# Two-head attention on one core: loads in halves, casts shared out and transposes moved in the first pair of heads

## The chip, the cores and the metric

The kernel runs on one core of a Trainium2 chip. The metric is the time of one execution in microseconds (us) of device time; lower is better. Three runs of the kernel before gave a median of 118.17 us (118.06 to 118.36). A separate execution was profiled: it took 117.7 us, of which the profile covers a span of 115.9 us; all times "at 5.19" in this document count from the start of that span.

## The reference

Softmax attention over 8 x 8 = 64 heads, 512 positions and 64 columns each, all in float32:

```python
def reference(q, k, v):                      # each (8, 8, 512, 64) float32
    scale = 1.0 / np.sqrt(q.shape[-1])
    scores = np.einsum('bhqd,bhkd->bhqk', q, k) * scale
    scores = scores - scores.max(axis=-1, keepdims=True)
    attn = np.exp(scores)
    attn = attn / attn.sum(axis=-1, keepdims=True)
    return np.einsum('bhqk,bhkd->bhqd', attn, v).astype(np.float32)
```

The inputs are drawn from a normal distribution with a fixed seed. The kernel leaves the subtraction of the maximum out, which changes nothing in exact arithmetic; it gets the row sums from a column of ones beside v.

## The kernel before, in words

Heads are worked on in 32 pairs (g = 0 to 31). For each pair one DMA each brings q, k and v (256 KB each, 128 partitions; a partition holds four neighbouring rows of each head, that is 1,024 contiguous bytes a head). Casts to float16 follow, mostly on POOL (GpSimd); PE (TensorE) transposes 128x128 blocks of q and k into PSUM, DVE (VectorE) copies these to SBUF, and PE multiplies them into scores. A *group* m is two score blocks of 128 keys by 512 queries, which share one of three PSUM buffers (st0, st1, st2). ACT (ScalarE) takes the exponential of a whole group in one instruction (128x1024, L594) and writes it to SBUF as float16. For 12 of the groups, from m = 11 on, DVE computes the exponential itself with a polynomial (L612, L634) so that ACT does not have to. PE then multiplies the exponentials with v (L683, "values"), and DVE normalises by the row sums (L655, L663) before the result is stored.

A class `Plan` simulates the engines once, with fixed costs and due times, when the program is built; the order of all steps after the start is its list. Each engine runs its own instructions strictly in the order of the program text, with semaphores between engines. The list that `Plan` makes is the same before and after the change.

The first pair (g = 0) is written by hand, in `first_loads` and `first_pair`. Its parts, which the prediction refers to:

- *Loads.* ACT's queue issues two loads of k (head 0, head 1; L727), SP's queue two loads of q (L728), each 128 KB. SP then goes on with the loads of the pairs 1 to 6 and part of 7 (L498), one after the other.
- *Casts.* q is cast into `q16` with every row written twice, side by side (`twice`), so that its transpose holds q in partitions 0 to 63 and again in 64 to 127. Head 0: q rows 0 and 1 on DVE (L746), k rows 0 and 1 on DVE (L747), q rows 2 and 3 on ACT (L748), k rows 2 and 3 on POOL (L749). Head 1: k on ACT (L750), q on POOL (L751). ACT loads its table of functions (L748, ACT_TABLE_LOAD) after it has issued its loads.
- *Fillers.* `busy` (L732) multiplies a constant, into a buffer that is overwritten later; it only keeps PE active. Six of 512 columns and two of 128 stand in front of the transposes, three of 128 in front of the first scores, and four of 128 in front of the scores of group 2.
- *Head 0.* Transposes of q blocks 0 and 1 into `tp_qa`, of k blocks 0 and 1 (L763; the first into `st_ka`, the second into buffer st1), of q blocks 2 and 3 into st1. Four DVE copies (L794 to L797) put them into `qt` and `kt`. Then the scores (L773): group 0 in two halves of 256 queries (`st_0a`, `st_0b`), each with an exponential of its own on ACT (L780), and group 1 (`st1`).
- *Head 1.* Four q transposes into `tp_qb`, two k transposes into `tp_kb`, the DVE copies L810 and L814, and the scores of group 2 (`st2`). The scores of group 3, the last of the pair, are the first step of `Plan`'s list (L589), followed by the transposes of pair 1 (L544, two times four), whose q half was cast in two parts on DVE (L512) and POOL (L513), the copies L551 and the scores of group 4, the first of pair 1.

Of the kernel before, what the change touches and what calls it, by code (L numbers as in the profile page):

```python
# [404 lines left out]
def kernel(  # L405
# [7 lines left out]
    nc = tc.nc  # L413
    B, H, S, D = q.shape
    P = 128
    NI = S // P
# [56 lines left out]
    def source(src, g):  # L473
        b, h = g // ppb, 2 * (g % ppb)
        return src[b, h : h + 2].rearrange("h (p i) d -> p h i d", i=NI)

    def load_tile(g, name):
        t = lpool.tile(
            [P, 2, NI, D],
            FP32,  # L480
            tag=f"{name}32",
            name=f"{name}32_{g}",
            bufs=7,
        )
        raw.setdefault(g, {})[name] = t
        return t
# [75 lines left out]
    def buffer(b, name):  # L562
        return ps_st.tile([P, 2, S], FP32, tag=f"st{b}", name=name)

    def scores(m, on_dve, b):
        grp = groups[m]
        half = m - len(groups) + 2
        cols = slice(256 * half, 256 * half + 256) if half >= 0 else slice(0, S)
        st = buffer(b, f"st_{m}")
        if on_dve:  # L570
            bits = dpool.tile([P, 2, S], U32, tag="pd", name=f"pd_{m}")
            pt = bits.bitcast(FP16).rearrange("p x (s n) -> p x s n", n=2)[:, :, :, 0]
            for x, (_, _, h) in enumerate(grp):
                s = slice(64 * h, 64 * h + 64)
                nc.tensor.matmul(st[:, x, :], lift[s], ones[s, 0:S], start=True, stop=False)
        elif half == 1:
            pt = last["pt"]
        else:
            pt = last["pt"] = ppool.tile([P, 2, S], FP16, tag="pt", name=f"pt_{m}")
        for x, (g, c, h) in enumerate(grp):  # L580
            if g == 0:
                s = slice(64 * (c % 2), 64 * (c % 2) + 64)
                kc = first["kt"][s, h, c // 2, :]
                qc = first["qt"][s, h].rearrange("p i c -> p (i c)")
            else:
                s = slice(64 * h, 64 * h + 64)
                kc = tqk[g][s, 1, c * P : (c + 1) * P]
                qc = tqk[g][s, 0, :]
            nc.tensor.matmul(st[:, x, cols], kc, qc[:, cols], start=not on_dve, stop=True)  # L589
            blocks[(g, c, h)] = pt[:, x, :]  # L590
        if on_dve:
            raised[m] = {"st": st, "bits": bits}
            return
        nc.scalar.activation(  # L594
            out=pt[:, :, cols], in_=st[:, :, cols], func=EXP, scale=scale
        )
# [126 lines left out]
    def first_loads():  # L723
        tk = load_tile(0, "k")
        tq = load_tile(0, "q")
        for h in range(2):
            nc.scalar.dma_start(out=tk[:, h], in_=source(k, 0)[:, h])  # L727
            nc.sync.dma_start(out=tq[:, h], in_=source(q, 0)[:, h])  # L728

    def busy(dst, n):  # L730

        nc.tensor.matmul(dst[:, 0:n], ones[:, 0:P], ones[:, 0:n], start=True, stop=True)  # L732

    def first_pair():


        tk, tq = raw[0]["k"], raw[0]["q"]
        k16 = cpool.tile([P, 2, NI, D], FP16, name="k16_0")
        q16 = cpool.tile([P, 2, NI, 2, D], FP16, name="q16_0")
        kt = cpool.tile([P, 2, 2, P], FP16, name="kt_0")  # L740
        qt = cpool.tile([P, 2, NI, P], FP16, name="qt_0")

        def twice(h, i, n):
            return tq[:, h, i : i + n].rearrange("p i (x d) -> p i x d", x=1).broadcast_to([P, n, 2, D])

        nc.vector.tensor_copy(out=q16[:, 0, 0:2], in_=twice(0, 0, 2))  # L746
        nc.vector.tensor_copy(out=k16[:, 0, 0:2], in_=tk[:, 0, 0:2])  # L747
        nc.scalar.copy(q16[:, 0, 2:4], twice(0, 2, 2))  # L748
        nc.gpsimd.tensor_copy(out=k16[:, 0, 2:4], in_=tk[:, 0, 2:4])  # L749
        nc.scalar.copy(k16[:, 1], tk[:, 1])  # L750
        nc.gpsimd.tensor_copy(out=q16[:, 1], in_=twice(1, 0, NI))  # L751

        pka, st1, st0 = (buffer(b, f"st_{n}") for b, n in enumerate(("ka", "1", "0a")))
        pqa = ps_x.tile([P, 8, P], FP16, tag="x0", name="tp_qa")
        pqb = ps_x.tile([P, 8, P], FP16, tag="x1", name="tp_qb")

        pka, pkc, pqc = pka[:, 0, :], st1[:, 0, :], st1[:, 1, :]
        pka, pkc, pqc = (
            t.bitcast(FP16).rearrange("p (n c) -> p n c", c=P) for t in (pka, pkc, pqc)
        )  # L760

        def t_k(dst, h, j):
            nc.tensor.transpose(  # L763
                dst, k16[:, h, 2 * j : 2 * j + 2, :].rearrange("p i d -> p (i d)"), ident
            )

        def t_q(dst, h, i):
            nc.tensor.transpose(dst, q16[:, h, i].rearrange("p x d -> p (x d)"), ident)

        def first_scores(st, h, j, q0, q1, pt, s0, s1):  # L770
            for x in range(2):
                s = slice(64 * x, 64 * x + 64)
                nc.tensor.matmul(  # L773
                    st[:, x, s0:s1],
                    kt[s, h, j, :],
                    qt[s, h].rearrange("p i c -> p (i c)")[:, q0:q1],
                    start=True,
                    stop=True,
                )
            nc.scalar.activation(  # L780
                out=pt[:, :, q0:q1], in_=st[:, :, s0:s1], func=EXP, scale=scale
            )

        for n in range(6):
            busy(st0[:, 0], S)
        for n in range(2):
            busy(st0[:, 0], P)
        for i in range(2):
            t_q(pqa[:, i], 0, i)
        t_k(pka[:, 0], 0, 0)  # L790
        t_k(pkc[:, 0], 0, 1)
        for i in range(2):
            t_q(pqc[:, i], 0, 2 + i)
        nc.vector.tensor_copy(out=qt[:, 0, 0:2], in_=pqa[:, 0:2])  # L794
        nc.vector.tensor_copy(out=kt[:, 0, 0], in_=pka[:, 0])
        nc.vector.tensor_copy(out=qt[:, 0, 2:4], in_=pqc[:, 0:2])
        nc.vector.tensor_copy(out=kt[:, 0, 1], in_=pkc[:, 0])  # L797
        for n in range(3):
            busy(st0[:, 1], P)
        pts = [ppool.tile([P, 2, S], FP16, tag="pt", name=f"pt_{m}") for m in range(3)]  # L800
        for m in range(3):
            for x, b in enumerate(groups[m]):
                blocks[b] = pts[m][:, x, :]
        first_scores(st0, 0, 0, 0, 256, pts[0], 0, 256)
        st0b = buffer(0, "st_0b")
        first_scores(st0b, 0, 0, 256, 512, pts[0], 0, 256)
        first_scores(st1, 0, 1, 0, S, pts[1], 0, S)
        for i in range(NI):
            t_q(pqb[:, i], 1, i)
        nc.vector.tensor_copy(out=qt[:, 1], in_=pqb[:, 0:4])  # L810
        pkb = ps_x.tile([P, 8, P], FP16, tag="x0", name="tp_kb")
        for j in range(2):
            t_k(pkb[:, j], 1, j)
        nc.vector.tensor_copy(out=kt[:, 1], in_=pkb[:, 0:2])  # L814
        st2 = buffer(2, "st_2")
        for n in range(4):
            busy(st2[:, 0], P)
        first_scores(st2, 1, 0, 0, S, pts[2], 0, S)
        first.update(kt=kt, qt=qt)

    with tc.manual_schedule():
        plan = Plan(groups, NP, 3)
        steps = plan.run()
        first_loads()
        for g, name in plan.first_loads:
            load(g, name)
# [5 lines left out]
        for n in range(NV):  # L832
            nc.vector.memset(vps[n][:, :, :, D : D + 1], 1.0)
        first_pair()
        do = {
            "transposes": transposes,
            "scores": scores,
            "values": values,
            "load": load,
# [43 lines left out]
```

## Time and profile before

| | |
|---|---|
| median of three runs | 118.17 us (118.06 to 118.36) |
| profiled execution, own time | 117.7 us |
| its span | 115.9 us |
| busy in the span: ACT, PE, DVE, POOL | 94%, 91%, 88%, 68% |
| first exponential (L780) starts | 5.19 us |
| fourth exponential (group 2, L780) starts | 7.48 us |
| last exponential ends | 112.60 us |

The profile's "busy" leaves out waiting and DMA issue. On PE, consecutive matmuls overlap in the records: one record covers the whole passage through the array, so the distance from start to start tells how fast they follow. "PEld" is PE's loading of weights, which runs beside its matmuls. The same holds for exponentials on ACT: one of 128x1024 is recorded with some 1.02 us, and the next starts 0.904 us after it.

### The profile page before, as it was taken

The page shows a single profiled execution, that of the slowest core. Times are in us where ns is not written, and L with a number is a line of the kernel's source. Part 1 is how long each engine was busy: PE and PEld are TensorE (multiplying, and loading weights), DVE is VectorE, ACT ScalarE, POOL GpSimd, SP SyncE. Part 2 cuts the span into 40 slices and gives each one's busy share as a digit, 9 for nine tenths or more (in the row PEclk, how much of TensorE's full clock was granted, in tenths as well). Part 3 has the DMA queues.
Part 4 walks back from the last instruction along what each step waited for, and adds up shares of the span by engine and source line. Part 5 has one row for each costly group of instructions (what it writes and reads, how often), then busy time and mean ns, then how long its engine had stood idle before and what let it go on. Part 6 is the DMA issues. An engine that isn't in the chain of part 4 may idle for free.

```text
span 115.9 us, 4106 instructions
## 1 busy us (share of the span) xinstructions
PE 105.8 (91%) x1583; PEld 67.1 (58%) x1583; DVE 101.6 (88%) x180; ACT 109.1 (94%) x121; POOL 78.9 (68%) x122
## 2 busy tenths in 40 slices
PE   7979997999989998899979999999999999899980
PEld 2546563657557565476655565765666665567660
DVE  4463599999999999999999999999999999999381
ACT  4499999999999999999999999999999999999980
POOL 2579870895995799676946999679995598740000
PEclk9999999999999999999999999999999999999999
DMA  3999999999999999999996899999999972035354
GB/s 105 326 373 378 384 380 382 383 376 322 343 367 338 306 362 385 369 378 354 316 296 210 264 320 343 294 312 369 328 306 314 332 269 94 0 96 184 95 187 133
DMA packets 35604, 33.83 MB, mean 292 GB/s; under 512 B 2688, under 2 KB 35584, under 8 KB 35584
## 3 DMA queue, kind: packets, MB, share of 16 engines
q1 hardware_dynamic: 35152, 33.24, 86.5%
q10 hardware_dynamic: 432, 0.33, 0.9%
q8 instruction: 12, 0.20, 0.7%
q14 instruction: 8, 0.07, 0.1%
HBM read 25.17 MB, written 8.39 MB: 289 GB/s over the span
## 4 chain that ended last, share of the span: by engine, by line
ACT 28%; PE 20%; DVE 15%; POOL 12%; issue 12%; DMA 8%; SPq 3%; POOLq 0%; ACTq 0%
ACT pt L594 27%; PE o L683 7%; PE st L589 6%; DMA v<-in_v_dram 5%; POOL qkp L519 5%; DVE ring L663 4%; POOL vp L504 3%; PE st_0a L732 3%; DMA out_dram<-ring 3%; DVE tqk L557 2%; DVE y L634 2%; DVE z L612 2%; DVE pd L634 2%; POOL t L647 2%; POOL k L517 2%
## 5 line engine op out<-in xcount | busy, mean ns | idle before, releaser
L594 ACT ACTIVATE pt<-st 128x1024 f16<-128x1024 f32 (+1 forms) x114 | 104.1, 1075 | 0.1
L589 PE MATMUL st<-tqk 64*128 64x512 f16 (+1 forms) x250 | 46.1, 381 | 4.2 <-ACT pt L594 3.1
L683 PE MATMUL o<-vp,pt 128*128 128x65 f16 x912 | 43.1, 194 | 0.7 <-DVE ring L663 0.6
L683 PEld LDWEIGHTS <-pt 128*128 128x128 f16 x912 | 35.6, 98 | 13.0 <-issue 10.3
L504 POOL CAST vp<-v 128x512 f16<-128x512 f32 x32 | 19.2, 616 | 10.4 <-DVE pd L634 5.9
L519 POOL CAST qkp<-k 128x512 f16<-128x512 f32 x31 | 21.0, 678 | 4.7 <-PE o L683 2.5
L663 DVE TENSOR_TENSOR ring<-o,rc 128x448 f32<-128x448 f32 (+2 forms) x37 | 22.6, 611 | 1.1
L589 PEld LDWEIGHTS <-tqk 64*128 64x128 f16 x250 | 13.2, 93 | 17.4 <-issue 8.7
L557 DVE COPY tqk<-tp 128x1024 f16<-128x1024 f16 x30 | 20.3, 676 | 3.0 <-PE tp L544 3.0
L519 POOL CAST qkp<-q 128x512 f16<-128x512 f32 x30 | 19.4, 646 | 4.4 <-DVE pd L634 4.0
L544 PE MATMUL tp<-ident,qkp 128*128 128x128 f16 x248 | 19.6, 219 | 0.8 <-DVE ring L663 0.5
L544 PEld LDWEIGHTS <-qkp 128*128 128x128 f16 x248 | 14.2, 97 | 8.4 <-issue 3.6
L634 DVE SCALAR_TENSOR_TENSOR pd<-y,z 128x1024 uint32<-128x1024 f32 x12 | 14.9, 1246 | 0.0
L612 DVE TENSOR_SCALAR z<-st 128x1024 f32<-128x1024 f32 x12 | 14.6, 1218 | 0.2 <-PE st L589 0.2
L634 DVE SCALAR_TENSOR_TENSOR y<-st,z 128x1024 f32<-128x1024 uint16 x12 | 14.6, 1215 | 0.0
L683 PE MATMUL o<-vp,pd 128*128 128x65 f16 x96 | 14.5, 194 | 0.0
L683 PEld LDWEIGHTS <-pd 128*128 128x128 f16 x96 | 9.4, 98 | 1.4 <-issue 1.2
L655 DVE RECIPROCAL rc<-o 128x7 f32<-128x7 f32 (+2 forms) x37 | 7.3, 197 | 2.9 <-PE o L683 2.6
L650 POOL TENSOR_TENSOR y<-t,y 128x1024 f32<-128x1024 f32 x4 | 9.5, 2364 | 0.3
L517 POOL TENSOR_SCALAR k<-k 128x128 f32<-128x128 f32 x12 | 6.3, 528 | 1.8 <-DVE pd L634 1.2
L634 DVE SCALAR_TENSOR_TENSOR y<-z,y 128x1024 f32<-128x1024 uint16 x4 | 5.4, 1344 | 0.0
L634 DVE SCALAR_TENSOR_TENSOR y<-st,y 128x1024 f32<-128x1024 uint16 x4 | 4.9, 1216 | 0.0
(53 smaller groups left out, 37.8 us busy)
## 6 DMA issues: line engine op xcount, KB each, us to landing
out_dram<-ring SPq DMA_DIRECT2D x63, 128.0 KB, 3.8
k<-in_k_dram SPq DMA_DIRECT2D x31, 256.0 KB, 5.1
q<-in_q_dram SPq DMA_DIRECT2D x31, 256.0 KB, 5.1
v<-in_v_dram SPq DMA_DIRECT2D x27, 256.0 KB, 4.8
v<-in_v_dram SPq DMA_DIRECT2D x10, 128.0 KB, 3.6
k<-in_k_dram ACTq DMA_DIRECT2D x2, 128.0 KB, 2.9
q<-in_q_dram SPq DMA_DIRECT2D x2, 128.0 KB, 2.7
out_dram<-obl SPq DMA_DIRECT2D x1, 64.0 KB, 1.6
```

Source lines behind the costliest of these rows:

```text
L504: return nc.gpsimd.tensor_copy(out=vps[g % NV][:, :, :, 0:D], in_=raw[g]["v"][:, :, :, :])
L517: ins = nc.gpsimd.tensor_scalar(out=x, in0=x, scalar1=LOG2E, scalar2=None, op0=AluOp.mult)
L519: ins = nc.gpsimd.tensor_copy(out=dst, in_=src[:, :, :, :])
L544: nc.tensor.transpose(tps[g][:, n, i, :], qkp[g][:, n, i, :], ident)
L557: nc.vector.tensor_copy(out=tqk[g][:, :, :], in_=tps.pop(g).rearrange("p n i c -> p n (i c)"))
L589: nc.tensor.matmul(st[:, x, cols], kc, qc[:, cols], start=not on_dve, stop=True)
L594: nc.scalar.activation(out=pt[:, :, cols], in_=st[:, :, cols], func=EXP, scale=scale)
L612: nc.vector.tensor_scalar(out=r["z"][:, :, :], in0=r["st"][:, :, :], scalar1=128.0, scalar2=2.0**17, op0=AluOp.mult, op1=AluOp.max,)
L634: nc.vector.scalar_tensor_tensor(out=r["bits"][:, :, :] if last else y, in0=(low, one, y)[s], scalar=(QUARTIC if shared else CUBIC)[s], in ...
L650: nc.gpsimd.tensor_tensor(out=y[:, :, :], in0=t[:, :, :], in1=y[:, :, :], op=AluOp.mult)
L663: nc.vector.tensor_tensor(out=ring[:, u % NU : u % NU + n, :], in0=o[:, x : x + n, 0:D], in1=rc[:, 0:n].broadcast_to([P, n, D]), op=AluOp. ...
L683: nc.tensor.matmul(os[u // 7][:, u % 7, :], blocks[(g, c, h)][:, y * P : (y + 1) * P], vps[g % NV][:, h, c, :], start=(c == 0), stop=(c == ...
```

## The change

In the first pair only, except for the fillers of group 4:

- The loads of head 0's q and k are cut in halves: rows 0 and 1, then rows 2 and 3 of each partition's four (64 KB, 512 bytes a partition), so that each of the two queues issues three loads where it issued two.
- Head 1's q is cast in two halves, rows 0 and 1 on POOL and rows 2 and 3 on ACT, where POOL cast all of it. On ACT this half stands in front of the cast of head 1's k.
- Head 1's first q transpose stands in front of the scores of group 0; its other three, and the two of k, stand behind group 0's scores and in front of group 1's, where all six stood behind group 1's.
- Fillers: one of 128 columns fewer in front of head 0's transposes, one fewer in front of the first scores, two fewer in front of group 2's; six new ones of 128 columns in front of group 4's scores.

```diff
@@ scores(m, on_dve, b)
+        if m == 4:
+            for n in range(6):
+                busy(st[:, 0], P)
@@ first_loads()
-        for h in range(2):
-            nc.scalar.dma_start(out=tk[:, h], in_=source(k, 0)[:, h])
-            nc.sync.dma_start(out=tq[:, h], in_=source(q, 0)[:, h])
+        for h, i, n in ((0, 0, 2), (0, 2, 2), (1, 0, 4)):
+            nc.scalar.dma_start(out=tk[:, h, i : i + n], in_=source(k, 0)[:, h, i : i + n])
+            nc.sync.dma_start(out=tq[:, h, i : i + n], in_=source(q, 0)[:, h, i : i + n])
@@ first_pair()
         nc.gpsimd.tensor_copy(out=k16[:, 0, 2:4], in_=tk[:, 0, 2:4])
+        nc.gpsimd.tensor_copy(out=q16[:, 1, 0:2], in_=twice(1, 0, 2))
+        nc.scalar.copy(q16[:, 1, 2:4], twice(1, 2, 2))
         nc.scalar.copy(k16[:, 1], tk[:, 1])
-        nc.gpsimd.tensor_copy(out=q16[:, 1], in_=twice(1, 0, NI))
...
         for n in range(6):
             busy(st0[:, 0], S)
-        for n in range(2):
-            busy(st0[:, 0], P)
+        for n in (P,):
+            busy(st0[:, 0], n)
...
-        for n in range(3):
+        for n in range(2):
             busy(st0[:, 1], P)
+        for i in range(1):
+            t_q(pqb[:, i], 1, i)
...
         first_scores(st0b, 0, 0, 256, 512, pts[0], 0, 256)
-        first_scores(st1, 0, 1, 0, S, pts[1], 0, S)
-        for i in range(NI):
+        for i in range(1, NI):
             t_q(pqb[:, i], 1, i)
-        nc.vector.tensor_copy(out=qt[:, 1], in_=pqb[:, 0:4])
         pkb = ps_x.tile([P, 8, P], FP16, tag="x0", name="tp_kb")
         for j in range(2):
             t_k(pkb[:, j], 1, j)
+        first_scores(st1, 0, 1, 0, S, pts[1], 0, S)
+        nc.vector.tensor_copy(out=qt[:, 1], in_=pqb[:, 0:4])
         nc.vector.tensor_copy(out=kt[:, 1], in_=pkb[:, 0:2])
         st2 = buffer(2, "st_2")
-        for n in range(4):
+        for n in range(2):
             busy(st2[:, 0], P)
         first_scores(st2, 1, 0, 0, S, pts[2], 0, S)
```

The order of instructions on DVE, and all that follows `Plan`'s list, stays as it was; SP's list gains one load at its head.

## The prediction

> **What bounds the kernel now.** First the page's busy table and its groups, then the timeline of ACT after the start:
>
> ```profile
> PE 105.8 (91%) x1583; PEld 67.1 (58%) x1583; DVE 101.6 (88%) x180; ACT 109.1 (94%) x121; POOL 78.9 (68%) x122
> L594 ACT ACTIVATE pt<-st 128x1024 f16<-128x1024 f32 (+1 forms) x114 | 104.1, 1075 | 0.1
> 27.62 84.98 ACT L594 ACTIVATE pt<-st 128x1024 f16<-128x1024 f32 x93
> ```
>
> ACT is the busiest engine, and its 114 exponentials of L594 have 0.1 us of idle time between them, all told. The last row is one unbroken stretch from 27.62 to 112.60. So ACT runs without a gap from its first L594 on, and the kernel ends a fixed tail after it. A change of the first pair is worth what it moves the start of that stretch. The chain of waits passes DVE, POOL and DMA rows between 47 and 100, but ACT has no idle row there: those engines run beside it with buffers between.
>
> Next, the timeline from 3 to 10, ACT first, then the engines that feed it:
>
> ```profile
> 3.33 0.40 ACT L748 CAST q<-q 128x256 f16<-128x256 f32 x1 [0.42 <-DMA q<-in_q_dram]
> 4.21 0.41 ACT L750 CAST k<-k 128x256 f16<-128x256 f32 x1 [0.47 <-DMA k<-in_k_dram]
> 5.19 0.60 ACT L780 ACTIVATE pt<-st_0a 128x512 f16<-128x512 f32 x1 [0.58 <-PE st_0a L773]
> 6.17 1.03 ACT L780 ACTIVATE pt<-st 128x1024 f16<-128x1024 f32 x1
> 7.48 1.02 ACT L780 ACTIVATE pt<-st 128x1024 f16<-128x1024 f32 x1 [0.29 <-PE st L773]
> ...
> 3.53 0.38 POOL L749 CAST k<-k 128x128 f16<-128x128 f32 x1 [2.25 <-DMA k<-in_k_dram]
> 3.99 0.61 POOL L751 CAST q<-q 128x512 f16<-128x512 f32 x1
> 6.05 0.40 POOL L513 CAST qkp<-q 128x256 f16<-128x256 f32 x1 [0.21 <-DMA q<-in_q_dram]
> ...
> 4.08 0.42 PE L768 MATMUL st<-ident,q 128*128 128x128 f16 x2
> 4.76 0.40 PE L773 MATMUL st_0a<-qt,kt 64*128 64x256 f16 x2
> 5.16 0.64 PE L773 MATMUL st<-qt,kt 64*128 64x512 f16 x2
> 5.73 0.60 PE L768 MATMUL tp_qb<-ident,q 128*128 128x128 f16 x4
> 7.05 0.39 PE L773 MATMUL st<-qt,kt 64*128 64x512 f16 x2 [0.19 <-DVE kt L814]
> 7.59 0.62 PE L544 MATMUL tp<-ident,qkp 128*128 128x128 f16 x8
> ```
>
> ACT's only holes lie here. The exponentials start at 5.19, 5.69, 6.17 and 7.48. A full one needs 0.92 before the next (7.48 to 8.40), so the fourth could start at 7.09; it is 0.39 late, since PE did group 1's scores (5.16), then six transposes (5.73 on), then two DVE copies, and group 2's scores only at 7.05. I forecast that fourth exponential. The trace's starts give PE's pace: transposes follow each other every 107 ns up to 6.55 and every 56 ns from 7.65; its clock record begins at 6.60.
>
> **The loads.** In the packet records 1,024 bytes take 46 ns and 512 bytes 27 ns (the last two stores), over 16 engines. Each of the two queues' first loads is read at 3.33 (q) and 3.53 (k), the second at 3.99 and 4.21. Of head 0, 256 packets become 512: (512 x 27 - 256 x 46) / 16 = 128 ns more. I take the transfers as bound by these packets, since engines were filled from 2.25 on. Then second halves are readable at 3.46 (q) and 3.66 (k), first halves 256 x 27 / 16 = 0.43 earlier, 3.03 and 3.23, and head 1 at 4.12 and 4.34. The bounds, however far: issued 1.6 us before landing, as the two 64 KB stores of the end were (k's second half at 1.15 + 1.6 = 2.75), or the second k load's time behind its issue, 4.21 - 1.15 = 3.06 (4.21). The packet sum lies between them and rests on the same transfers, so I take it. [...]
>
> Each queue issues one load more, 0.43 each. On ACT this moves the table load from 1.63 to 2.06, done at 3.34, before its data at 3.46. On SP all later loads go out 0.43 later; pair 1's k and q took 3.6 to 3.9 us from issue to reading behind queued packets, so I charge them 0.13, and at worst 0.43. Pair 1's q (POOL L513, now 6.05) is then cast by 6.9; its PE transposes come at about 7. This costs nothing.
>
> **Head 0 in front of the first scores.** One filler less ends PE's fillers at 3.38. DVE casts q 3.03 to 3.32 and k 3.24 to 3.46; q transposes at 3.38 and 3.49 (now 3.68), k's first at 3.59. All of that is early, but PE then stops for the second half of k: POOL casts it 3.66 to 4.04 (0.38), the transpose starts at 4.11 where it started at 3.98, and q 2 and 3 follow at 4.21 and 4.32, 0.13 late. The first half's 0.3 us is thus hidden behind this wait.
>
> Next in PE's order are two fillers (4.43, 4.54) and the moved transpose. It waits for POOL's half cast, 4.12 to 4.52 by the 0.40 of L513; queued behind it is everything on PE, the first scores above all. At 4.64 it is ready, and the first scores start at 4.75, as now (4.76). The second half of group 0 waits for DVE's `qt` copy: transposes end at 4.32 + 0.31, copy 4.66 to 4.95, scores 5.00 (now 4.945). The first exponential stays at 5.19.
>
> **Five transposes in front of group 1.** From 5.00, 0.21 for the scores, then five transposes of 0.107: 5.21 to 5.75. ACT's two casts are done for them: q half 4.12 to 4.52, k 4.42 to 4.83, and both end before the exponential at 5.19. Group 1's scores begin at 5.75 instead of 5.16, take 0.63 to the end of the record, and its exponential starts at 6.41 instead of 6.17: a loss of 0.24. In return the copies start early: `qt` 5.77 to 6.19, `kt` 6.11 to 6.39, group 2's scores at 6.45 instead of 7.05. They end by 7.08 at the slow pace, so ACT is late next: 6.41 + 0.92 = 7.33 instead of 7.48. **Sum: -0.15.**
>
> **What must follow.** Group 3 reuses buffer 0, free at 6.3. Group 4 now starts its exponential at 9.31 with its scores done at 9.23; pair 1's transposes move with group 2's scores, 7.59 to about 7, so it keeps pace. Six fillers there cost 6 x 0.056 = 0.34 after transposes that end at 7.6, while the copies L551 need until 8.2: nothing; without that cover 0.34. All stays shifted if nothing later eats it.
>
> 117.7 - 0.15 = 117.55 against the profiled execution, which lies 0.47 below the median; 118.17 - 0.15 = **118.02**. A difference of 0.3% is 0.35 us, about what a measurement of this kernel can tell from no change.
>
> **Rivals.**
>
> *Loads come early: faster.* The fourth exponential follows k's second half R: 7.33 - 3.66, so R + 3.67, as long as head 1 keeps ahead. R = 3.46 gives 0.35. With the 1.6 us of the stores, fillers until 3.38 would be the limit: transposes to 3.92, first scores after two fillers and one transpose at 4.35, second half 4.58, group 1's exponential at 6.00, the fourth at 6.92: -0.56, 117.61. For: half the bytes first. Against: the first loads took 2.6 to 3.0 us, not 1.6.
>
> *Loads cost time from their issue: slower.* If each piece needs 3.06 from its own issue, k's second half (issued 1.15) is readable at 4.21, and PE's whole order waits for it: 4.21 + 3.67 = 7.88, +0.40, 118.57. It decides for slower by 0.3% from 4.16 on, and leaves no gain from 3.81 on. Head 1's q has the same effect through the moved transpose: read at L, first scores at L + 0.56, the fourth exponential 2.52 later; even at L = 4.40, +0.35 at 4.75. For: both k loads had nearly one delay from issue (2.82, 3.06). Against: engines were full then, and half the data is in front.
>
> *PE stays slow for longer: slower.* PE would stand at about 3.7 to 4.1 for k. At the slow pace group 3's scores begin at 6.88, the eight transposes at 7.31 to 8.17, the second copy ends at 8.83, group 4's exponential comes at 9.55 against 9.31: +0.25, and up to +0.5 as the backlog of transposes grows. [...]
>
> *The gain is eaten later: no change, 118.17.* ACT's starts have stretches of 0.93 to 1.1 instead of 0.904 around the groups that DVE raises; they move along unless loads in absolute time bind.
>
> **How the numbers follow.** Forecast 0.37 and eaten 0.07, both within 0.3%: 0.44. Early loads 0.32. Late loads 0.15, slow PE 0.09: 0.24. The range goes from 117.5 (the early end, 0.1 more) to 118.6 (late loads).
>
> **What would show it.** In the profile after: casts of first halves near 3.03 and 3.23; POOL's k cast near 3.66; first scores near 4.75; exponentials at 5.19, 6.41 and 7.33, without idle time before the next. It is wrong if the fourth exponential does not move by about what the time does, if POOL's k cast starts later than 3.8, or if transposes behind 7 still come every 107 ns.

## The result and the profile after

The kernel after took 118.90 us (median of six runs, 118.85 to 119.58), the kernel before 117.93 (median of six, 117.53 to 118.36): a ratio of 1.0109, interval 1.0073 to 1.0145. It is 1.1% slower, 0.97 us by the medians, where 0.15 us less was forecast (118.02, with a range up to 118.6). Run again beside other kernels it gave 1.0107 (1.0068 to 1.0146), 1.0041 (1.0004 to 1.0079) and 1.0068 (1.0034 to 1.0102). The profiled execution took 118.89 us, span 117.1, against 117.7 and 115.9. The ratios leave out executions that lie more than 1.5% above the fastest of their kernel; medians and the table further down count all.

First two lines of the page after: busy times, and ACT's group of exponentials (L597 is L594 of before; busy, mean ns, idle time before them):

```profile
PE 107.1 (91%) x1585; PEld 67.4 (58%) x1585; DVE 101.4 (87%) x180; ACT 109.5 (93%) x122; POOL 78.5 (67%) x122
L597 ACT ACTIVATE pt<-st 128x1024 f16<-128x1024 f32 (+1 forms) x114 | 104.1, 1078 | 0.5 <-PE st L592 0.5
```

ACT's work is the same 104.1; its idle time rose from 0.1 to 0.5, all of it waiting for scores. The timeline of ACT after the change has the place:

```profile
4.51 0.41 ACT L754 CAST q<-q 128x256 f16<-128x256 f32 x1 [0.69 <-DMA q<-in_q_dram]
5.65 0.60 ACT L784 ACTIVATE pt<-st_0a 128x512 f16<-128x512 f32 x1 [0.43 <-PE st_0a L777]
7.05 1.94 ACT L784 ACTIVATE pt<-st 128x1024 f16<-128x1024 f32 x2 [0.32 <-PE st L777]
8.88 1.03 ACT L597 ACTIVATE pt<-st 128x1024 f16<-128x1024 f32 x1
10.36 103.21 ACT L597 ACTIVATE pt<-st 128x1024 f16<-128x1024 f32 x113 [0.45 <-PE st L592]
```

The first exponential is 0.46 late (5.65 against 5.19). The row at 7.05 merges groups 1 and 2; their starts are 7.05 and 7.97, so the fourth exponential is 0.49 late (7.48 before). Group 4's starts at 10.36 instead of 9.31, 1.05 late, and from there one unbroken row of 113 runs to the end, as before. So the loss is 0.49 in front of group 2 and 0.56 between groups 2 and 4, and ACT gets nothing back.

The timelines of POOL and PE after the change show where each part comes from:

```profile
3.48 0.29 POOL L752 CAST k<-k 128x128 f16<-128x128 f32 x1 [2.20 <-DMA k<-in_k_dram]
4.54 0.40 POOL L753 CAST q<-q 128x256 f16<-128x256 f32 x1 [0.77 <-DMA q<-in_q_dram]
...
4.12 0.42 PE L735 MATMUL st_0a<-const-bfloat16-1.0 128*128 128x128 bf16 x2
5.00 0.29 PE L772 MATMUL tp_qb<-ident,q 128*128 128x128 f16 x1 [0.46 <-POOL q L753]
5.22 0.40 PE L777 MATMUL st_0a<-qt,kt 64*128 64x256 f16 x2
5.76 0.50 PE L772 MATMUL tp_qb<-ident,q 128*128 128x128 f16 x3
6.40 0.61 PE L777 MATMUL st<-qt,kt 64*128 64x512 f16 x2
8.24 1.04 PE L544 MATMUL tp<-ident,qkp 128*128 128x128 f16 x8
```

Head 1's q is read at 4.54 on POOL where it was read at 3.99. PE's fillers stream until 4.34 (two of 107 ns from 4.12); the moved transpose starts at 5.00, and the scores stand behind it. The last row is the second part: the eight transposes of pair 1 take 1.04 where they took 0.62, 107 ns from start to start. PE's clock is still at half pace there; its record begins at 10.05 instead of 6.60. (The granted-clock column shows 1.00 even here, because the record covers nothing before the clock opens; the distances tell it.) In what follows the clock is called open from the start of its record on, when 128 columns pass in 56 ns instead of 107, and closed before it. A *window* is a stretch of 3.41 that ends at an opening, or a whole number of times 3.41 away from one: in the run with the held load (below) the clock was closed again for 3.41 (12.15 to 15.56), and it was open for 109.23 in the profile before (6.60 to 115.82) and for 105.81 in the one after (10.05 to 115.86), 32 and 31 times 3.413. That the clock goes by such stretches is my reading of these distances.

Page part 6 has the loads of pair 0 (KB each, median us from issue to landing): cut in half they are quick, the third one is not.

```profile
k<-in_k_dram ACTq DMA_DIRECT2D x2, 64.0 KB, 2.2
q<-in_q_dram SPq DMA_DIRECT2D x2, 64.0 KB, 2.1
q<-in_q_dram SPq DMA_DIRECT2D x1, 128.0 KB, 2.9
```

### The profile page after: what moved, and what is told of

It reads as the page before. It is cut to its first block, busy times and chain, and to the rows that moved or that the text cites. A ratio compares the mean times of both kernels' runs of the same rounds, so it can differ in the third digit from the quotient of the medians.

```text
span 117.1 us, 4115 instructions
## 1 busy us (share of the span) xinstructions
PE 107.1 (91%) x1585; PEld 67.4 (58%) x1585; DVE 101.4 (87%) x180; ACT 109.5 (93%) x122; POOL 78.5 (67%) x122
## 4 chain that ended last, share of the span: by engine, by line
ACT 24%; PE 17%; DVE 16%; DMA 15%; POOL 13%; issue 11%; SPq 1%; POOLq 0%; ACTq 0%
ACT pt L597 24%; DMA q<-in_q_dram 9%; PE st L592 6%; PE o L686 5%; DVE ring L666 5%; POOL qkp L519 4%; DMA v<-in_v_dram 3%; POOL vp L504 3%; PE tp L544 3%; DVE pd L637 3%; DMA out_dram<-ring 2%; POOL y L653 2%; DVE z L615 2%; POOL t L650 2%; DVE tqk L557 2%
## 5 line engine op out<-in xcount | busy, mean ns | idle before, releaser
L597 ACT ACTIVATE pt<-st 128x1024 f16<-128x1024 f32 (+1 forms) x114 | 104.1, 1078 | 0.5 <-PE st L592 0.5
L519 POOL CAST qkp<-q 128x512 f16<-128x512 f32 x30 | 20.4, 679 | 4.7 <-DMA k<-in_k_dram 4.3
L519 POOL CAST qkp<-k 128x512 f16<-128x512 f32 x31 | 19.9, 643 | 4.8 <-PE o L686 1.3
L637 DVE SCALAR_TENSOR_TENSOR pd<-y,z 128x1024 uint32<-128x1024 f32 x12 | 15.4, 1285 | 0.0
```

Of the source, the lines that this page charges most:

```text
L519: ins = nc.gpsimd.tensor_copy(out=dst, in_=src[:, :, :, :])
L597: nc.scalar.activation(out=pt[:, :, cols], in_=st[:, :, cols], func=EXP, scale=scale)
L637: nc.vector.scalar_tensor_tensor(out=r["bits"][:, :, :] if last else y, in0=(low, one, y)[s], scalar=(QUARTIC if shared else CUBIC)[s], in ...
```

## The experiments

Ratios are to the kernel before, run on the same chip. The kernel after ran on three of the five chips, but not on the two where its parts were put back and its stop was first filled; its own ratios, 1.0041 to 1.0109, are what those runs have to be held against.

**The stop filled.** Of the kernel after:

```diff
-        for n in range(2):
+        for n in range(8):
             busy(st0[:, 1], P)
         for i in range(1):
             t_q(pqb[:, i], 1, i)
```

> Of the kernel after, PE's stop in front of the moved transpose (from 4.34 to 5.00) is filled with six more fillers of 128 columns (6 x 0.107 = 0.64). Clock theory: the stop left the window that ends near 6.6 too idle, so PE's clock stayed at half speed until 10.05. Filled, transposes come every 56 ns from about 6.6 on; the first exponential stays late at about 5.65, but group 4's starts at about 9.8 instead of 10.36, with no idle time before it: about 0.5 to 0.6 below the kernel after, 0.4 to 0.5 above the kernel before. Rival (the late loads alone set the time, the clock only shows it): no change against the kernel after, 1.0 above the kernel before.

118.44 us, ratio 1.0011 (0.998 to 1.0042): the loss was gone. The profile shows another way to it than expected: the clock opened at 3.46 already, and groups 2 to 4 came 1.81 apart. Head 1's q was read at 4.97, later still.

> The kernel after with its stop filled by six more fillers, as in the run with the filled hole, now beside the kernel after itself. Clock theory: 0.4 to 0.7 below the kernel after of these runs, clock open at 3.4 or 6.8 instead of 10, group 4's exponential 0.5 or more sooner against the first one. Rival (the late loads set the time): within 0.2 of the kernel after.

118.87 us, ratio 1.0098 (1.0069 to 1.0127), against 1.0107 for the kernel after beside it: no gain. In its profile all the loads were later (first head's ACT cast at 3.78 instead of 3.42), PE stopped for k instead (0.45 by the profile's row, at 4.36), the fillers then reached up to the moved transpose at 5.50, and the clock opened at 10.05. The two runs of one kernel contradict each other and decide nothing between the two theories; a fixed number of fillers does not fill a stop whose place and length vary.

**One part put back at a time.** First the moved transpose, of the kernel after:

```diff
-        for i in range(1):
-            t_q(pqb[:, i], 1, i)
...
-        for i in range(1, NI):
+        for i in range(NI):
             t_q(pqb[:, i], 1, i)
```

> Of the kernel after, head 1's first q transpose is put back behind group 0's scores, with the other three; the loads stay in three pieces. Wait theory: only the moved transpose makes the first scores wait for the late q of head 1 (4.51). Without it the first scores start near 4.4, ACT is then held by its two casts until about 5.15, and the fourth exponential comes at about 7.2 (7.97 after, 7.48 before); PE stands little, the clock opens near 6.6: 0.2 to 0.3 below the kernel before, 1.2 below the kernel after. Rival (loads in three pieces cost by themselves, whatever PE's order): still 0.4 or more above the kernel before.

118.62 us, ratio 1.0017 (0.9977 to 1.0057). Most of the loss is gone, not with a gain as expected. In its profile head 1's q came at 5.18, PE stopped before the four transposes instead, and the clock opened at 10.12.

> The kernel after with head 1's first q transpose put back behind group 0's scores, a second time, on this chip. In the first run head 1's q was read at 5.18, so PE stood all the same, for all four transposes. Loads theory: the three-piece loads bring head 1's q at 4.5 to 5.2 and wherever its transposes stand in front of group 1 PE stops for them; 0.5 to 1.2 above the kernel before. Rival (the moved first transpose alone is at fault): within 0.3 of the kernel before or below.

118.61 us, ratio 1.0047 (1.0013 to 1.0081), 0.55 above the kernel before, as the loads theory had it. Its profiled execution, of 117.37 us, caught another case: q at 4.39, clock open at 5.06. ACT's timeline there:

```profile
4.39 0.40 ACT L754 CAST q<-q 128x256 f16<-128x256 f32 x1 [0.56 <-DMA q<-in_q_dram]
4.70 0.40 ACT L755 CAST k<-k 128x256 f16<-128x256 f32 x1
5.00 0.59 ACT L784 ACTIVATE pt<-st_0a 128x512 f16<-128x512 f32 x1
7.78 104.27 ACT L597 ACTIVATE pt<-st 128x1024 f16<-128x1024 f32 x114
```

The first exponential starts as soon as ACT's casts let it, at 5.00, no gap follows, and group 3 starts at 7.78 (8.40 before). This one execution kept its early front to the end; by the median of its twelve the kernel gains nothing.

Then the loads alone, put back in the kernel after:

```diff
-        for h, i, n in ((0, 0, 2), (0, 2, 2), (1, 0, 4)):
-            nc.scalar.dma_start(out=tk[:, h, i : i + n], in_=source(k, 0)[:, h, i : i + n])
-            nc.sync.dma_start(out=tq[:, h, i : i + n], in_=source(q, 0)[:, h, i : i + n])
+        for h in range(2):
+            nc.scalar.dma_start(out=tk[:, h], in_=source(k, 0)[:, h])
+            nc.sync.dma_start(out=tq[:, h], in_=source(q, 0)[:, h])
```

> Of the kernel after, only the loads are put back to one a head; casts, order and fillers stay changed. Wait theory: head 1's q is read at 3.99 again, POOL's half cast is done at 4.4, PE comes to the moved transpose at 4.5 without a stop, first scores at about 4.65, fourth exponential at about 7.2, clock open near 6.6: 0.2 to 0.3 below the kernel before. Rival (five transposes in front of group 1, or ACT's extra cast, cost the time): at or above the kernel before, group 1's exponential after 6.6.

118.03 us, ratio 0.9975 (0.9942 to 1.0008): the time is what was expected. The profiled execution (119.58 us) is not: PE did not stop for head 1's q, but group 1's exponential started at 6.65 and the fourth at 7.57, where 7.2 was expected. That is the sign that the rival named, so the five transposes do cost something.

> The kernel after with one load a head, a second time, on this chip. Loads theory: within 0.4 of the kernel before, about 1 below the kernel after's ratio of 1.011; head 1's q read near 3.9, clock open at the first or second window. Rival (the order of transposes or the extra cast on ACT carries the loss): 0.8 or more above the kernel before.

118.36 us, ratio 1.0050 (1.0019 to 1.0080): 0.6 above the kernel before, more than the 0.4 expected. In the profiles of the two runs head 1's q was read at 3.88 and 3.77, and PE did not stop for it. The second profile shows ACT's cast, then the moved transpose right behind PE's fillers:

```profile
3.77 0.41 ACT L754 CAST q<-q 128x256 f16<-128x256 f32 x1 [0.24 <-DMA q<-in_q_dram]
4.08 0.42 PE L735 MATMUL st_0a<-const-bfloat16-1.0 128*128 128x128 bf16 x2
4.30 0.31 PE L772 MATMUL tp_qb<-ident,q 128*128 128x128 f16 x1
4.54 0.28 PE L777 MATMUL st_0a<-qt,kt 64*128 64x256 f16 x2
9.23 103.65 ACT L597 ACTIVATE pt<-st 128x1024 f16<-128x1024 f32 x113 [0.53 <-PE st L592]
```

The fourth exponential came at 6.74, yet group 4's only at 9.23 (last row; 9.31 before), since pair 1's q was read on DVE at 7.39. With the first transpose put back as well (this diff and the one before it):

> Both put back: one load a head, and head 1's first transpose behind group 0's scores; casts on two engines, five more places in front of group 1 and fillers stay as after. Loads theory: no PE stop, as with the loads alone put back; first exponential at 5.0 to 5.2, the fourth near 7.5; within 0.4 of the kernel before. If the moved first transpose costs by itself: 0.1 to 0.3 below the kernel with the loads alone put back.

118.22 us, ratio 1.0044 (1.0010 to 1.0078), 0.5 above the kernel before and again more than expected, with the fourth exponential at 6.88. Against 1.0050 beside it, no cost of the moved transpose by itself can be told when q is there.

By ratio these runs overlap with the lowest ones of the kernel after. Over all timed executions, chips mixed, the medians are 118.02 us for the kernel before (110), 119.04 for the kernel after (36), 118.12 with the loads put back (36, three runs) and 118.61 with the first transpose alone put back (24). So the loads carry nearly all of the loss, and while they are late the moved transpose makes some 0.4 of it.

And the other way: the kernel before with the loads of the kernel after (the last diff reversed), nothing else:

> Of the kernel before, only the loads are cut in halves. Wait theory: the first head's part comes earlier, nothing on PE waits for head 1's q before group 1's scores; head 1's q, cast whole on POOL, is ready at about 5.15, its transposes at 5.2 as PE comes to them; the first exponential is held by ACT's cast of k until about 5.1; the fourth exponential at 7.1: 0.1 to 0.4 below the kernel before. Rival (later loads cost by themselves): 0.4 or more above.

118.70 us, ratio 1.0062 (1.0022 to 1.0102): 0.7 above, which is what the rival expected. The front came early, though less than expected: fourth exponential at 7.30, 0.18 sooner. It was given back, in ACT's timeline:

```profile
8.22 4.68 ACT L594 ACTIVATE pt<-st 128x1024 f16<-128x1024 f32 x5
13.17 36.35 ACT L594 ACTIVATE pt<-st 128x1024 f16<-128x1024 f32 x39 [0.26 <-PE st L589]
50.07 10.26 ACT L594 ACTIVATE pt<-st 128x1024 f16<-128x1024 f32 x11 [0.55 <-PE st L589]
```

ACT stops at 12.9: the group that starts at 13.17 is the first of pair 2, whose q cast began at 10.15 there and at 8.64 before. With the loads put back pair 2's q cast began at 9.59 on the same chip, so not all of the lateness is the halves'; but the early front was worth nothing, since the next pairs' data did not come sooner with it.

**The loads by themselves.** In the kernel after, SP's loads of pair 1 and later were issued behind DVE's first cast:

```diff
+        held = nc.vector.tensor_copy(out=q16[:, 0, 0:2], in_=twice(0, 0, 2))
+        for n, (g, name) in enumerate(plan.first_loads):
+            ins = load(g, name)
+            if n == 0:
+                tc.add_manual_dep(ins.ins, held.ins.name, SYNC, reason="hold")
```

> Of the kernel after, SP's first load of pair 1 is made to wait for the end of DVE's first cast (about 3.05) where it went out at 2.10, and all later loads with it; a probe of the third loads. If pair 1's load on SP's queue takes the engines' time from them, head 1's q is read at about 4.1 instead of 4.51 and its k at about 4.3 instead of 4.79. If they cost time from their own issue (1.63 plus 2.8 to 3.1), they stay at 4.4 to 4.8. The time itself is worse in any case, since all later loads are 1.0 later.

119.86 and 121.83 us. Head 1's q was read at 4.27 and its k at 4.58, between the two expectations. This decides nothing: in its four profiles the unchanged kernel after reads q at 4.24 to 4.55. What all profiles show is the issue. With three loads on a queue head 1's q is issued at 1.61 to 1.63 instead of 1.14 to 1.16, and lands 2.60 to 3.54 behind its issue (ten profiles) against 2.57 to 2.79 (six). So some 0.47 of the lateness is the one more issue in front, 0.49 of 0.55 in the profile after; the rest varies between nothing and 0.9, and its cause stays open.

ACT stopped 1.2 us before pair 2's first group (14.16). PE had waited 0.89 for that pair's cast, and the clock, open from 5.32, closed again from 12.15 to 15.56 (the page's row of the granted clock, 40 slices):

```profile
PEclk9999589999999999999999999999999999999999
```

So little is in hand for later loads; how much of that stop is the closed clock's stays open.

**The clock by itself.** In the kernel before, first without the later fillers:

```diff
-        for n in range(3):
-            busy(st0[:, 1], P)
...
-        for n in range(4):
-            busy(st2[:, 0], P)
```

> Of the kernel before, the three fillers in front of the first scores and the four in front of group 2's are left out; loads, casts and order stay. Clock theory: PE is busy for some 70% of the window that ends near 6.6 instead of 86%, the clock stays at half speed until about 10; the first exponential comes no later than 5.19, yet group 4's starts at 9.8 or later instead of 9.31: 0.4 to 0.7 above the kernel before. Rival (fillers are idle decoration): no change, or 0.1 below since the first scores start 0.1 sooner.

117.92 us, ratio 1.0001 (0.9965 to 1.0038): no loss. The profiled execution did not test the theory, since its window lay from 1.49 to 4.91, with the six large fillers in it, and the clock opened at 4.91. Four of the twelve timed executions have their window, by the reckoning below, about where the profiled execution of before has it; their median is 118.16, 0.3 above the five of the kernel before there on the same chip (117.83), where 0.4 to 0.7 was expected. That is too few to tell. Then without any filler, these too:

```diff
-        for n in range(6):
-            busy(st0[:, 0], S)
-        for n in range(2):
-            busy(st0[:, 0], P)
```

> Of the kernel before, all fillers of the first pair are left out, so that PE is idle until head 0's first cast; loads, casts and order stay as before. Clock theory, for a clock that opens late with loads as before: at most 65% of a window that ends near 6.6 is busy, the clock stays at half speed until about 10 whatever the place of the window; the time from group 2's to group 4's exponential is 2.2 to 2.5 as in the kernel after, not 1.83, and the time is 0.4 to 0.6 above the kernel before. Rival (the closed clock costs nothing by itself): within 0.2 of the kernel before.

119.80 us, ratio 1.0136 (1.0078 to 1.0193), more than the whole change, with loads, casts and order as before. ACT's timeline:

```profile
4.96 0.60 ACT L780 ACTIVATE pt<-st_0a 128x512 f16<-128x512 f32 x1 [0.42 <-PE st_0a L773]
7.54 1.02 ACT L780 ACTIVATE pt<-st 128x1024 f16<-128x1024 f32 x1 [0.58 <-PE st L773]
10.06 3.77 ACT L594 ACTIVATE pt<-st 128x1024 f16<-128x1024 f32 x4 [0.59 <-PE st L589]
14.84 100.00 ACT L594 ACTIVATE pt<-st 128x1024 f16<-128x1024 f32 x109 [1.00 <-PE st L589]
```

The first exponential is 0.23 sooner and the fourth within 0.06 of before, yet group 4's is at 10.06 instead of 9.31, and pair 2's first group stops ACT for another 1.0: here the clock opened at 15.25. Data were not what PE waited for: pair 2's q was cast by 9.82, and PE came to that pair's transposes at 10.81. A closed clock costs by itself, here 1.6 where 0.4 to 0.6 was expected.

**Does the loss hang on where the window lies?** The kernel after ran three times more, unchanged:

> The kernel after once more, unchanged, beside the other three on one chip. Chain theory (late head 1 q, PE's stop, closed clock): again 0.8 to 1.2 above the kernel before; head 1's q read at 4.5 or later, first exponential at 5.6 or later, clock open only near 10. If the loss was particular to the first chip: within 0.3 of the kernel before.

> The kernel after, unchanged, for more executions. Window theory: the 3.41 us window of the clock lies differently in each execution. From each timed run's span and granted clock the place of its boundaries follows, modulo 3.41. With boundaries at 2.5 to 3.4 the kernel after opens its clock near 10 where the kernel before opens it near 6.6: 118.6 to 119.6. With boundaries at 1.1 to 2.0 (a window from about 1.5 to 4.9, nearly full in both) it opens near 5: 117.9 to 118.5, within 0.8 of the kernel before there (117.6). Below 1.0 both open late: 118.6 to 119.2, as the kernel before. Rival (the late loads set the time, the clock only shows it): no relation to the place of the window, 118.8 to 119.2 everywhere.

> The same kernel once more, for the same count: what is expected by the place of the window is as in the run beside it.

119.11, 118.97 and 119.09 us (ratios above). The first profile repeated the chain: q read at 4.55, first exponential 5.69, clock open at 9.60. The second, of 117.77 us, shows the kernel after with its clock open at 4.44:

```profile
4.43 0.41 ACT L754 CAST q<-q 128x256 f16<-128x256 f32 x1 [0.62 <-DMA q<-in_q_dram]
5.41 0.60 ACT L784 ACTIVATE pt<-st_0a 128x512 f16<-128x512 f32 x1 [0.26 <-PE st_0a L777]
6.38 1.95 ACT L784 ACTIVATE pt<-st 128x1024 f16<-128x1024 f32 x2
8.19 104.27 ACT L597 ACTIVATE pt<-st 128x1024 f16<-128x1024 f32 x114
```

The first exponential is late as ever (5.41), but the five transposes now pass at 56 ns, no gap is left, and group 3 starts at 8.19, sooner than before's 8.40. The same kernel and nearly the same late load: the two profiled executions, 118.89 and 117.77 us, differ by 1.1 with the clock.

The third profile, of 120.94 us, is a miss of the expectation. By the place of its window the clock was to open near 10; it opened at 6.00. Head 1's q was read at 4.24, so that PE stood for less, and its window was streaming for 77%. (Streaming is the time in which columns pass: 107 ns for 128 of them while the clock is closed, 56 ns while it is open.) The fourth exponential came at 7.45 and group 3's at 8.36, about as before; the time went in four later stops of ACT, between 49 and 97, 2.2 us in all. So the place of the window alone does not tell when the clock opens: the one in front of 6.00 streamed for 77%, the one in front of 6.63 in the profile after, which left the clock closed, for 65%.

The ends of the windows are called boundaries in what follows. For the timed runs a boundary's place is an estimate from the span and the mean granted clock, for an execution whose clock closes again only after PE's last work, as in the profiles before and after (0.5 granted from 115.82 and 115.86 on, PE's last matmul started at 112.76 and 113.73): the closing lies (1 - clock) x 2 x span before the end, and boundaries are taken to recur every 3.413, a 32nd of the 109.23 (to about 0.12). These are all runs whose place can be worked out this way (from five chips); a clock of 1.000 gives no place (33 executions of before, 10 of after, 13 with the loads put back):

| boundaries, modulo 3.413 | before | after | loads put back (three runs above) |
|---|---|---|---|
| 0 to 1.0 | 118.94 (13) | 119.04 (6) | 118.86 (8) |
| 1.0 to 2.3 | 117.68 (26) | 119.17 (3: 117.77, 119.17, 120.66) | 117.93 (8) |
| 2.3 to 3.41 | 118.09 (32) | 119.12 (17) | 118.13 (7) |

(median us, count). With boundaries from 2.3 on, where the profiled executions of before and after lie (6.60 and 10.05 are 3.19 and 3.22 modulo 3.413), the change costs 1.0 us and putting the loads back takes all of that away. The other two rows can't be read like this, because a run has a place only if its clock closes before it ends. With boundaries below 1.0 the closing mostly comes 116.0 to 117.0 after the start, so that the row holds long executions of whatever kernel; the one profile in it (the stop filled the first time) opened its clock at 3.46, early. In the middle class it depends on the end too: the profiles at 1.03 and 1.41 closed at 113.67 and 114.05, those at 1.06 and 1.49 at 117.11 and 117.55, behind their spans. For the kernel after that leaves three runs, of which one agrees with what was expected. So the timed runs do not show that the loss hangs on the place of the window: the kernel after has 119.04 to 119.17 in all three rows, as the rival expected. What speaks for the clock's share are the profiles and the run without fillers.

## Why the prediction was wrong

**The bound** was right: ACT is gapless from group 4 on in both, and group 4's shift, 1.05, covers that of the time. Last exponentials end 0.97 apart (10.36 + 103.21 against 112.60), the medians 0.97 too. The two profiled executions differ by 1.2, since the tail behind the last exponential, taken as fixed, took 3.55 against 3.31. Of the three signs of being wrong two came: the fourth exponential moved by 0.49 and the time by 0.97, and transposes behind 7 still came every 107 ns.

**The failing step: the loads, "I take the transfers as bound by these packets".** It was mis-sized in both directions. The second halves came a little sooner than forecast (k's cast at 3.48, not 3.66), though their packets of 512 bytes again took 27 ns, but head 1's q, the third load, was read at 4.51 instead of 4.12. Over all profiles head 1's q is read at 4.24 to 5.18 with three loads a queue and at 3.77 to 3.99 with two. The engines were not as full then: the packets carry 0.25 MB between 3 and 4 at a DMA share of 0.92, against 0.29 and 1.03 before, and 1.19 MB by 6.0 against 1.32. Head 1's q landed 2.86 behind its issue (1.63 + 2.86 = 4.49), where the second load of before took 2.79 from an issue at 1.14. So the rival "loads cost time from their issue" had the third piece right, but it was priced by k's second half, which came early; its 3.06 was never added to the third load's own issue (1.63 + 3.06 = 4.69).

**Head 0 in front of the first scores** was right up to there. Then the moved transpose, forecast at 4.64, stood at 5.00, and the first scores at 5.22 instead of 4.75: the term that I sized at nothing cost 0.46. Its neighbours were named ("queued behind it is everything on PE").

**Five transposes in front of group 1** lacked a cost. From the start of the first scores to group 1's exponential I summed 1.66; it took 1.83. PE's rows have it: where PE goes from whole-array transposes to the 64-row scores or back, 0.14 passes beyond the streaming (5.40 + 0.21 = 5.61, next at 5.76; 6.16 + 0.11 = 6.27, next at 6.40), and the new order has two more such turns. The row of before showed it too (5.16 + 0.43 = 5.59, next at 5.73). So even with q in time and the clock as before, the forecast 7.33 would have been about 7.5, no gain; the first profile with the loads put back, clock open at 6.46, has 7.57.

**"PE stays slow for longer"**, at 0.09, is what happened, with its price: +0.25 to +0.5 forecast, 0.56 measured between groups 2 and 4. What failed is my estimate of PE's idle time. Before, PE stood 0.2 (3.48 to 3.68) and 0.14 (4.62 to 4.76) in front of the opening; I took some 0.5 for after, and that this would be little enough for the clock to open was an estimate too, which no run shows. PE stood 1.2 us in the window from 3.22 to 6.63 (0.66 of it before the moved transpose), which was streaming for 65%; in before's window, from 3.18 to 6.60, for 86%. I weighed the late q and the slow clock as separate cases; here they are one, since PE's wait for q is more than half of the idle time in the window that left the clock closed.

All profiles bear this out. Group 2 to group 4 takes 1.80 to 1.83 in the nine where the clock opened before 7 and pair 1's data were there; 2.25 to 2.52 in the five where it opened at 9.6 or later. Two with an early clock have 2.5 (later fillers left out, and loads put back the second time): pair 1's data came late there, with k cast only at 6.77 and 6.17 and DVE's part of q at 7.42 and 7.39, against 5.23 and 6.91 before. By the starts of PE's matmuls the windows at whose end the clock opened streamed for 75 to 95%, those that left it closed for up to 76%.

**Fillers of group 4**: right at full pace, hidden. At half pace they end at 9.71, under the copy L551 that ends at 9.74: still hidden, with nothing to spare.

**Eaten later** was too small a case. In eight profiles the fourth exponential came before 7.48; six of them met a stop of ACT at group 4 or later, and two kept what they had without one (117.37 and 117.77 us). The kernels with the loads put back still stand at 0.9975 to 1.0050.

## What to carry to other kernels

A step moved in front of the first useful work takes over that work's latest input: before moving it, put the latest arrival that the traces allow into its place, not the expected one, and count every load issued in front of it (here one more, 0.47). A stop of PE near the start can cost more than itself: here 0.46, and 0.56 more through the clock, which stayed closed at the end of a window that streamed for 65% and opened at 10.05, where before it opened at 6.60 behind one with 86%. So add up PE's idle time there, and weigh a late input and a slow clock as one case. An early start is worth only as much as the loads of the next steps have in hand.

## What the runs showed of the hardware

- The clock's openings and closings lay whole steps apart: 12.15 to 15.56 in the run with the held load is one of 3.41 us, 6.60 to 115.82 before are 32 of 3.413, 10.05 to 115.86 after are 31. I had not expected how far the steps shift from one execution to the next: the profiles here open at 3.46 to 15.25, and the same kernel after at 4.44, 6.00, 9.60 and 10.05.
- How full the windows were: 86% streaming in the one in front of 6.60 before, 77% in the one in front of 6.00 in the profile of 120.94 us, 75 to 95% in all at whose end the clock opened; 65% in the one of after that left the clock closed, and up to 76% in others that did (the shares are worked out from the starts of PE's matmuls).
- A third load on a queue at the start (128 KB) landed 2.9 us after its issue in the profile after, and 2.6 to 3.5 over ten profiles; the 64 KB ones in front of it took 2.1 to 2.2 in the profile after. Where q has two loads of 128 KB, the second took 2.6 to 2.8 (six profiles).
